# Values of heads 0 to 7 as products 512 columns wide, the second quarter of them kept on the chip

## The chip, the cores and the metric

The kernel runs on one core of a Trainium2 chip. A core has five engines, each with a queue of its own: TensorE (PE in the profile; its weight loads are listed apart as PEld), VectorE (DVE), ScalarE (ACT), GpSimd (POOL) and SyncE (SP, which here only starts transfers). Matrix products are accumulated in PSUM, eight banks of 512 float32 columns by 128 partitions; everything else lives in SBUF. The metric is the time of one execution on the device in microseconds (us); less is better. The profile is that of one execution, its times counted from the first instruction.

## The reference

One layer is applied to 128 prompt tokens and 512 latent tokens with the same weights, 1024 channels wide. Per token:

```
h = x * (1 + scale) + shift                       # modulation from the condition
z = h @ w_in                                      # 1024 -> 10240
v_h, x1, x0 : short convolution of z; y_h = (longconv(v_h * x1) + skip) * x0
q, k, v     : 16 heads of 64; prompt: full attention;
              latents: 2-D window plus the cached context keys, one softmax
p_h = (y_h * silu(g_h)) @ w_bh;  p_a = (y_a * silu(g_a)) @ w_ba
out = (sigmoid(m_h) * p_h + sigmoid(m_a) * p_a) @ w_out
x_new = layer_norm(alpha * x + gate * out)
```

Outputs are the new tokens of both groups and the prompt's keys and values (new_k, new_v). The change concerns `v = h @ w_v`, 640 tokens by 1024 columns, of which 64 columns are one head.

## The kernel before

**Precision.** Every float32 operand of a large product is split in a high part, rounded to the type that TensorE takes at full rate, and the low rest. A product is three products: high by high, low by high, high by low. The tokens are `hH` and `hL` (eight tiles of 128 channels by 640 tokens each), the weights `wh` and `wl`.

**Weight supply.** A weight tile is 128 partitions by 1024 columns (512 KB). `wtile` (L144) makes one ready: SyncE loads it into a ring `raw` of three; ScalarE writes its negative, rounded, into `wl` (L156, ring of three); GpSimd starts a second transfer of the same tile that adds to `wl` (L157), which leaves the rest with its sign; ScalarE writes `wh` (L158, ring of two). A ring's next tile is written only when the last reader of the old one is done.

**Stages.** Projections for the long convolution and the convolution itself (in four quarters) come first, then what the code calls the hand-over, then attention, whose query, key, gate and mixing weights go through `pair_tile` (a scheme with seven products of half size, L1167), then the output projections and the normalisation. The hand-over, `hand_over` (L943), makes the last gated convolution rows, then the values of all heads and the first query and key tile. Beside it runs the last quarter's long convolution (transforms `long_conv`, `long_conv_back`, and `gated_conv`, which ends with transposes `y`), then `attention_setup` (L956), which frees the convolution's memory and opens attention's, then `late_sums` (L793), sums of token tiles that `pair_tile` takes as operands. `weave` (L73) interleaves the two in the order in which they are written into the program: a piece of the side after so many pieces of the main, at 81 main pieces to 28 side pieces.

**Who orders what.** In the hand-over a planner orders every engine's instructions: it simulates the program with its own costs and sends ahead what is ready. From attention on (the block that opened with `values_back(1)` at L1335) TensorE's order is that of the program, and the planner orders the others. Each engine takes its queue in order.

**Values.** `values(m)` (L898) makes four heads, 256 columns, for m = 0 to 3. For each of eight channel tiles it multiplies the stationary token tile (128 channels by 128 tokens) with 256 weight columns, for five tiles of 128 tokens and three products: 120 products of 256 columns, at L917 (token tiles 0 to 3, two to a PSUM bank) and L929 (token tile 4). PSUM is used through two pools of four banks, `acc` (main, L104) and `aux` (L101), each handed out in turn. ScalarE copies the sums out (L924: two of 512 columns; L931: one of 256). For m = 0 they go to the place from which attention reads them, `slot(0, "v")`. The place of m = 1, in the pool `slots_r`, is only opened after the hand-over (L1280); those of 2 and 3 are still in use by others until far into attention. So m = 1, 2, 3 are copied into the room of the first keys (`k`, `kl` of `slots_l`), stored to DRAM (`v_d`, three transfers each), and read back by `values_back(m)` (L937): m = 1 at the start of attention, ahead of the first load of the output gate's weights (`gate_load`), the others later. The order of the hand-over is values 1, 2, 3, queries 0, keys 0, values 0.

The first use of a value in attention is well after its start: the first blocks compute scores (L979) and softmax first.

Of the kernel before, what the change touches and what calls it, by code (L numbers as in the profile page):

```python
# [11 lines left out]
AF = mybir.ActivationFunctionType  # L12
# [34 lines left out]
def tile_hyena_natten_step(ctx: ExitStack, tc: tile.TileContext, a, o):  # L47
# [751 lines left out]
    def alongside(main, side, every, first=0):  # L799
        for i, _ in enumerate(main):  # L800
            if i >= first and i % every == 0:
                next(side, None)
            yield
        for _ in side:
            pass

    at = sp = tp = None

    with tc.manual_schedule(engines={mybir.EngineType.PE, mybir.EngineType.DVE, mybir.EngineType.Activation}):
        prologue()  # L810
# [22 lines left out]
    def slot(j, tag, name, dt=F32):  # L833
        pool = out["slots_l" if j % 2 == 0 else "slots_q" if tag[0] == "q" else "slots_r"]
        return pool.tile([P, SLOT[tag]], dt, tag=tag, name=name)
# [62 lines left out]
    def values(m):  # L898
        w = [wtile(T_V + 2 * m + i, "dma", width=256) for i in range(2)]
        ps = [acc(f"v{m}_{i}") for i in range(2)]  # L900
        if m:
            v = [slot(0, t, f"v{m}{t}")[:, :n] for t, n in (("k", 512), ("kl", 768))]
            v = [v[0], v[1][:, :512], v[1][:, 512:]]
        else:
            out["v0"] = slot(0, "v", "v0")
            v = [out["v0"][:, 512 * i : min(512 * i + 512, 1280)] for i in range(3)]

        def passes(k):
            wh, wl = w[k // 4][0][k % 4], w[k // 4][1][k % 4]
            return ((hH, wh, k == 0, False), (hL, wh, False, False), (hH, wl, False, k == NK - 1))  # L910

        for half in range(2):
            ks = range(4 * half, 4 * half + 4)
            for k in ks:
                for x, wk, first, last in passes(k):
                    for t in range(4):
                        nc.tensor.matmul(  # L917
                            ps[t // 2][:, t % 2 * 256 : t % 2 * 256 + 256], x[:, k, P * t : P * t + P], wk,
                            start=first and t % 2 == 0, stop=last, skip_group_check=True,
                        )  # L920
                yield
            if half:
                for i in range(2):
                    nc.scalar.activation(v[i], ps[i][:], AF.Copy)  # L924
            else:
                pe = acc(f"ve{m}")
            for k in ks:
                for x, wk, first, last in passes(k):
                    nc.tensor.matmul(pe[:, :256], x[:, k, P * 4 :], wk, start=first, stop=last, skip_group_check=True)  # L929
            yield  # L930
        nc.scalar.activation(v[2], pe[:, :256], AF.Copy)  # L931
        nc.sync.dma_start(o["new_v"][:, m * 256 : m * 256 + 256], v[0][:, :256])
        for i in range(3 if m else 0):
            nc.sync.dma_start(v_d[m][:, 512 * i : min(512 * i + 512, 1280)], v[i])
        yield

    def values_back(m):  # L937
        out[f"v{m}"] = slot(m, "v", f"v{m}")
# [4 lines left out]
    def hand_over():  # L943
        nonlocal tp
        yield from quarter_tail(3)
        hwa_stack.close()
        out["slots_l"] = left.enter_context(tc.tile_pool(name="slots_l", bufs=1))
        out["slots_q"] = left.enter_context(tc.tile_pool(name="slots_q", bufs=1))
        tp = left.enter_context(tc.tile_pool(name="tp", bufs=1))
        yield from alongside(chain(values(1), values(2), values(3), queries(0), keys(0), values(0)), early_sums(), 1)  # L950

    tail = ctx.enter_context(ExitStack())
    ac = ctx.enter_context(ExitStack())
    edges, biases = {}, {}

    def attention_setup():  # L956
        nonlocal at, sp
        while "early_sums" not in out:
            yield
        hy.close()  # L960
        sp = ac.enter_context(tc.tile_pool(name="sp", bufs=1, side="right"))
        at = ac.enter_context(tc.tile_pool(name="at", bufs=1, side="right"))
        biases[0] = [bias_tile(h) for h in range(2)]
        for b, c in ((0, 0), (3, 320)):
            for h in range(2):
                edges[b, h] = at.tile([P, 384], F32, tag=f"edge{b}{h}", name=f"edge{b}{h}")
                nc.gpsimd.memset(edges[b, h][:, c : c + 64], 0.0)
        yield
# [273 lines left out]
    def mix_(m):  # L1242
# [10 lines left out]
    GATED_AT = [runs[0][i][0] for i in (0, 1, 2, 3, 5, 6, 7, 8, 10, 11, 12, 13, 15, 16, 17, 18)]  # L1253

    weave(hand_over(), chain(gated_conv(2), long_conv(3), long_conv_back(3), gated_conv(3), attention_setup(), late_sums()),
          4 * NK + 3 * N_VALUES + 16, 2 * N_GATED + N_CONV + N_BACK + 7)
    gp = left.enter_context(tc.tile_pool(name="gp", bufs=1))
    gbc = gp.tile([P, 2, D], F32, tag="gbc", name="gbc")

    gate_raw, gate_n = {}, [0]  # L1260
# [7 lines left out]
    def gate_row(after):  # L1268
# [6 lines left out]
        behind(ins, after)  # L1275
        tc.keep_in_program_order(ins)
        gate_n[0] += 1

    rs = left.enter_context(ExitStack())
    out["slots_r"] = rs.enter_context(tc.tile_pool(name="slots_r", bufs=1))  # L1280

    def yh_home(i):
        if i < 4:
# [48 lines left out]
        }[j]  # L1332

    with tc.manual_schedule(engines={mybir.EngineType.PE}):
        values_back(1)  # L1335
        before = last[0]
        gate_load()
        behind(last[0], before)
        for j in range(8):
            main, n_main = mains(j)  # L1340
            if j in (3, 5):
                values_back(j // 2 + 1)
            weave(chain(*main), attend(j), n_main, N_ATT if j < 7 else N_ATT + 3, 1 if j in (2, 4, 6) else 0)
# [284 lines left out]
def _layout(inp):  # L1628
    g = {n: np.asarray(v) for n, v in inp.items()}
    x = np.concatenate([g["x_prompt"][0], _to_blocks(g["x_sample"][0])], axis=0)  # L1630

    def ktiles(w):
        n = w.shape[1] // 128
        return w.reshape(8, 128, n, 128).transpose(2, 1, 0, 3).reshape(n, 128, 1024)

    w_in = g["w_in"][0]
    w_v = w_in[:, 48 * 128 : 56 * 128].reshape(2, 4, 128, 4, 256).transpose(3, 0, 2, 1, 4).reshape(8, 128, 1024)
    wall = np.concatenate(
        [ktiles(w_in[:, : 48 * 128]), w_v, ktiles(w_in[:, 56 * 128 :]), ktiles(g["w_bh"][0]), ktiles(g["w_ba"][0]), g["w_out"][0].reshape(8, 128, 1024)], axis=0)
    b_ada = g["b_ada"][0]  # L1640
    w3 = g["filt_w3"][0].reshape(64, 2, 4, 256).transpose(0, 2, 1, 3).reshape(64, 4, 512)
    b1, b2 = g["filt_b1"][0], g["filt_b2"][0]
    fr = g["filt_freq"][0]
    fs2 = np.stack([b2, fr[1]], axis=1)
    w2 = g["filt_w2"][0]
    convw = np.concatenate([g["conv_w"][0], g["conv_b"]], axis=0).reshape(4, 24, 128).transpose(2, 1, 0)
    p, n = np.arange(128)[:, None], np.arange(256)[None]
    ri = (n % 64) // 8 - (p % 64) // 8 + 7
    ci = np.clip((n // 64) * 8 + n % 8 - 8 - (p // 64) * 8 - p % 8 + 15, 0, 30)
    rpbT = g["rpb"][0][:, ri, ci]  # L1650
    half, qc8 = np.arange(128) // 64, np.arange(128) % 8
    qc = half * 8 + qc8
    bias = np.zeros((16, 128, 1024))
    for w, lo, r0, cols in (
        (24, np.maximum(qc - 8, 0), 64, (slice(0, 192),)), (32, qc, 0, (slice(320, 448), slice(576, 704))),
        (24, 8 + np.minimum(qc - 8, 0), 0, (slice(832, 1024),)),
    ):
        j = np.arange(8 * w)
        key = (j // 64) * 8 + j % 8
        ok = (key[None] >= lo[:, None]) & (key[None] < lo[:, None] + 16)  # L1660
        part = np.where(ok[None], rpbT[:, :, r0 : r0 + 8 * w], -BIG)
# [15 lines left out]
    return {n: np.ascontiguousarray(v) for n, v in out.items()}  # L1677
# [33 lines left out]
```

## Time and profile before

| | |
|---|---|
| median of three runs | 863.28 us (860.81 to 864.22) |
| the profiled execution | 860.83 us |
| its span (first to last instruction) | 859.1 us |
| granted clock of TensorE, mean | 0.998 of full |
| products of `values`, first and last start | 298.1 and 382.3 us (L917, L929) |
| values(0), the last part of the hand-over | 368.3 to 382.4 us |

In a list of groups or of instructions, `v<-wl,hH` is output and inputs; `128*128 128x256` is the shape of a product, here 128 channels by 128 tokens stationary and 256 columns moving; `x128` is the count. A product's duration is from its start to the modelled end of its results; products overlap, so the distance between starts tells what one costs in a row of them. A bracket at a line's end is the time for which the engine sat idle before it and what ended that. In the chain of work that ended last each piece carries only the time that it added. A queue's own row (SPq) is the issue of a transfer, not the transfer.

### The profile page before, as it was taken

Reading aid. Unit: us, or ns where it says so; the run is one execution under the profiler, and the core shown is the slowest. Engines: PE = TensorE matmul, PEld = TensorE weight load, DVE = VectorE, ACT = ScalarE, POOL = GpSimd, SP = SyncE. Lnnn points to the kernel's source line nnn. Section 1 sums busy time; section 2 is a strip of 40 time slices with the busy share of each in tenths; the row PEclk is TensorE's granted clock in tenths of the full one; section 3 lists DMA queues with packets and bytes.
Section 4 is the critical chain, followed back from the end, with each engine's and each line's share of the span. In section 5 each row is a group of like instructions: output and inputs, shape, how many; then the busy total and the mean of one; then the engine's idle time right before and its main releaser. Section 6 shows DMA issues by size and latency. Waiting matters only on the chain.

```text
span 859.1 us, 16817 instructions
## 1 busy us (share of the span) xinstructions
PE 849.4 (99%) x6387; PEld 822.7 (96%) x6387; DVE 678.7 (79%) x1408; ACT 464.7 (54%) x996; POOL 131.4 (15%) x140
## 2 busy tenths in 40 slices
PE   9999999999999999999999999999999999999996
PEld 7999999999999999999999999999999999999885
DVE  6777695697759559789988897889888778799776
ACT  4675656545554643646665676666655654345310
POOL 0010010101001010105232225124222200000000
PEclk9999999999999999999999999999999999999999
DMA  9986575656657558774263535354354386445621
GB/s 352 359 256 144 109 149 126 153 122 144 127 134 150 126 146 187 168 251 148 85 195 90 192 95 189 106 177 149 105 173 118 111 266 202 173 131 140 246 107 54
DMA packets 56868, 138.64 MB, mean 161 GB/s; under 512 B 8495, under 2 KB 23859, under 8 KB 56788
## 3 DMA queue, kind: packets, MB, share of 16 engines
q1 hardware_dynamic: 45412, 111.69, 39.7%
q0 software_dynamic: 5760, 20.19, 14.4%
q10 hardware_dynamic: 5616, 5.70, 1.9%
q8 instruction: 50, 0.82, 0.4%
q14 instruction: 30, 0.25, 0.1%
HBM read 121.43 MB, written 16.12 MB: 160 GB/s over the span
## 4 chain that ended last, share of the span: by engine, by line
PE 95%; DMA 3%; DVE 1%; SPq 0%; ACT 0%; issue 0%; DVEq 0%
PE sp L1182 33%; PE mm L177 30%; PE out L1534 6%; PE v L917 5%; PE pt L1019 3%; PE s L1026 3%; PE s L979 2%; PE mm L191 2%; PE ve L929 1%; DMA raw<-wall 1%; DMA wl<-wall 1%; DMA ada<-wada 1%; PE adaT L262 1%; PE yb L166 1%; PE yb L165 1%; PE yb L167 1%
## 5 line engine op out<-in xcount | busy, mean ns | idle before, releaser
L1182 PE MATMUL sp<-t,wb 128*128 128x320 f32 x912 | 141.7, 310 | 0.0
L1182 PEld LDWEIGHTS sp<-t,wb 128*128 128x128 f32 x912 | 134.9, 188 | 0.9 <-ACT pp L1047 0.5
L1182 PE MATMUL sp<-hH,wb 128*128 128x320 f32 x456 | 111.2, 314 | 0.0
L177 PE MATMUL mm<-hH,wl 128*128 128x320 f32 x448 | 105.5, 309 | 0.1
L177 PE MATMUL mm<-hH,wh 128*128 128x320 f32 x448 | 104.9, 309 | 0.0
L177 PE MATMUL mm<-hL,wh 128*128 128x320 f32 x448 | 104.2, 310 | 0.0
L157 POOL DMA_DIRECT2D wl<-wall x37 | 32.2, 870 | 329.5 <-ACT wl L156 263.3
L108 ACT ACTIVATE wb<-s 128x512 fp32r<-128x512 f32 x92 | 56.3, 627 | 45.6 <-DVE s L1142 26.6
L1182 PEld LDWEIGHTS sp<-hH,wb 128*128 128x128 f32 x456 | 78.4, 188 | 2.3 <-issue 2.1
L158 ACT ACTIVATE wh<-raw 128x1024 fp32r<-128x1024 f32 x37 | 39.2, 1059 | 70.8 <-PE mm L177 65.3
L177 PEld LDWEIGHTS mm<-hH,wl 128*128 128x128 f32 x448 | 75.5, 188 | 0.9 <-DMA wl<-wall 0.4
L177 PEld LDWEIGHTS mm<-hH,wh 128*128 128x128 f32 x448 | 75.2, 188 | 0.5
L177 PEld LDWEIGHTS mm<-hL,wh 128*128 128x128 f32 x448 | 75.1, 188 | 0.3
L109 DVE TENSOR_TENSOR wb<-s,wb 128x512 fp32r<-128x512 f32 x92 | 62.5, 692 | 10.3 <-ACT wb L108 10.3
L1182 PE MATMUL sp<-hL,wb 128*128 128x320 f32 x228 | 70.4, 309 | 0.0
L108 ACT ACTIVATE wb<-raw 128x512 fp32r<-128x512 f32 x66 | 41.4, 628 | 44.4 <-PE sp L1182 23.5
L1001 POOL TENSOR_SCALAR p<-p,sm 128x384 f32<-128x384 f32 x32 | 44.5, 1399 | 102.7 <-DVE sm L1000 102.7
L109 DVE TENSOR_TENSOR wb<-raw,wb 128x512 fp32r<-128x512 f32 x66 | 46.6, 705 | 5.5 <-ACT wb L108 5.4
L177 PE MATMUL mm<-yhs,wh 128*128 128x320 f32 x256 | 47.9, 309 | 0.0
L1197 DVE TENSOR_TENSOR c<-sp,u 128x320 f32<-128x320 f32 x69 | 33.5, 486 | 12.0 <-PE sp L1182 12.0
L1182 PEld LDWEIGHTS sp<-hL,wb 128*128 128x128 f32 x228 | 42.8, 188 | 0.0
L1001 POOL TENSOR_SCALAR edge<-edge,sm 128x320 f32<-128x320 f32 x32 | 41.9, 1318 | 0.5 <-DVE sm L1000 0.5
(385 smaller groups left out, 2078.3 us busy)
## 6 DMA issues: line engine op xcount, KB each, us to landing
raw<-wall SPq DMA_DIRECT2D x93, 512.0 KB, 3.6
wl<-wall POOLq DMA_DIRECT2D x37, 512.0 KB, 5.8
ada<-wada SPq DMA_DIRECT2D x16, 512.0 KB, 9.2
tm<-bias SPq DMA_DIRECT2D x16, 512.0 KB, 4.5
xw<-xw SPq DMA_DIRECT2D x8, 512.0 KB, 9.4
gate<-wgate SPq DMA_DIRECT2D x8, 512.0 KB, 4.1
wo<-wall SPq DMA_DIRECT2D x8, 512.0 KB, 5.3
dec<-decay SPq DMA_DIRECT2D x20, 128.0 KB, 3.0
```

Of the source, the lines that this page charges most:

```text
L108: hi = nc.scalar.activation(dst_h, src, AF.Copy)
L109: return hi, (eng or nc.vector).tensor_tensor(dst_l, src, f(dst_h), op=ALU.subtract)
L157: nc.gpsimd.dma_start(wl, a["wall"][i], accum_op=ALU.add)
L158: nc.scalar.activation(wh, raw[:], AF.Copy)
L177: nc.tensor.matmul(ps[hf][:, :HALF], wt[k], x[:, hf * HALF : (hf + 1) * HALF], start=(i == 0 and k == 0), stop=(i == lead[2] and k == NK - ...
L917: nc.tensor.matmul(ps[t // 2][:, t % 2 * 256 : t % 2 * 256 + 256], x[:, k, P * t : P * t + P], wk, start=first and t % 2 == 0, stop=last, ...
L1001: nc.gpsimd.tensor_scalar_mul(pv, pv, sm[:, 2:3])
L1019: nc.tensor.transpose(pt[:, i * P : i * P + P], x, ident)
L1026: nc.tensor.matmul(dst, lhs, rhs, start=start, stop=stop, skip_group_check=True)
L1182: nc.tensor.matmul(dst, wk, x(xi, k), start=j < 4 and k == 0 and i == 0, stop=k == 3 and i == 2, skip_group_check=True,)
L1197: after = nc.vector.tensor_tensor(c, dst, c if j == 3 else u, op=ALU.add)
L1534: ins = nc.tensor.matmul(dst, m[k][:, c0 : c0 + P], w[:, c : c + n], start=(first and k == 0), stop=(last and k == 5), skip_group_check=True,)
```

## The change

`values` stays for m = 2 and 3 only. A new part, `first_values`, at the end of the hand-over, makes heads 0 to 7 (512 columns) at once: four weight tiles hold two channel tiles by 512 columns each (the host lays out the weights so), and for each weight tile and each of five token tiles there are six products of 512 columns: two channel tiles by three. The five sums stay open in PSUM through all four weight tiles, four in the main pool's banks and one in an `aux` bank; after the last weight tile's products for a token tile, ScalarE copies its two halves to the places of m = 0 and m = 1. For this, `slots_r`, and `gp` (the output gate's rows) which lies before it in memory, are opened in `attention_setup`, within the hand-over. The stores of m = 1 to DRAM and its load go. The weave's ratio is again 81 to 28 (written as a number), but the main part now has its last 20 pieces in `first_values`, of which 9 lie past the 81, where before the 11 pieces of values(0) did.

```diff
     def values(m):
         w = [wtile(T_V + 2 * m + i, "dma", width=256) for i in range(2)]
         ps = [acc(f"v{m}_{i}") for i in range(2)]
-        if m:
-            v = [slot(0, t, f"v{m}{t}")[:, :n] for t, n in (("k", 512), ("kl", 768))]
-            v = [v[0], v[1][:, :512], v[1][:, 512:]]
-        else:
-            out["v0"] = slot(0, "v", "v0")
-            v = [out["v0"][:, 512 * i : min(512 * i + 512, 1280)] for i in range(3)]
+        v = [slot(0, t, f"v{m}{t}")[:, :n] for t, n in (("k", 512), ("kl", 768))]
+        v = [v[0], v[1][:, :512], v[1][:, 512:]]
...
-        for i in range(3 if m else 0):
+        for i in range(3):
             nc.sync.dma_start(v_d[m][:, 512 * i : min(512 * i + 512, 1280)], v[i])
         yield
+
+    def first_values():
+        ps = {}
+        for kt in range(4):
+            w = wtile(T_V + kt, "dma", width=512)
+            for t in range(5):
+                if kt == 0:
+                    ps[t] = acc(f"v_{t}") if t < 4 else aux("ve")
+                for n, (x, i, kk) in enumerate(((hH, 0, 0), (hL, 0, 0), (hH, 0, 1), (hL, 0, 1), (hH, 1, 0), (hH, 1, 1))):
+                    nc.tensor.matmul(
+                        ps[t][:], x[:, 2 * kt + kk, P * t : P * t + P], w[i][kk],
+                        start=kt == n == 0, stop=kt == 3 and n == 5, skip_group_check=True,
+                    )
+                if kt == 3:
+                    while "slots_r" not in out:
+                        yield
+                    for m in range(2):
+                        if t == 0:
+                            out[f"v{m}"] = slot(m, "v", f"v{m}")
+                        v = out[f"v{m}"][:, 256 * t : 256 * t + 256]
+                        nc.scalar.activation(v, ps[t][:, 256 * m : 256 * m + 256], AF.Copy)
+                        if t == 0:
+                            nc.sync.dma_start(o["new_v"][:, m * 256 : m * 256 + 256], v)
+                yield
...
-        yield from alongside(chain(values(1), values(2), values(3), queries(0), keys(0), values(0)), early_sums(), 1)
+        yield from alongside(chain(values(2), values(3), queries(0), keys(0), first_values()), early_sums(), 1)
...
     def attention_setup():
...
         at = ac.enter_context(tc.tile_pool(name="at", bufs=1, side="right"))
+        gp = left.enter_context(tc.tile_pool(name="gp", bufs=1))
+        rs = left.enter_context(ExitStack())
+        out["slots_r"] = rs.enter_context(tc.tile_pool(name="slots_r", bufs=1))
...
-          4 * NK + 3 * N_VALUES + 16, 2 * N_GATED + N_CONV + N_BACK + 7)
-    gp = left.enter_context(tc.tile_pool(name="gp", bufs=1))
+          81, 2 * N_GATED + N_CONV + N_BACK + 7)
...
-        values_back(1)
-        before = last[0]
         gate_load()
-        behind(last[0], before)
```

More of the change, by code (lines that the diff above doesn't have):

```diff
@@ L805, in alongside @@
             pass
-    at = sp = tp = None
+    at = sp = tp = gp = rs = None
     with tc.manual_schedule(engines={mybir.EngineType.PE, mybir.EngineType.DVE, mybir.EngineType.Activation}):
@@ L956, in attention_setup @@
     def attention_setup():
-        nonlocal at, sp
+        nonlocal at, sp, gp, rs
         while "early_sums" not in out:
@@ L1277, in gate_row @@
         gate_n[0] += 1
-    rs = left.enter_context(ExitStack())
-    out["slots_r"] = rs.enter_context(tc.tile_pool(name="slots_r", bufs=1))
     def yh_home(i):
@@ L1636, in _layout @@
     w_in = g["w_in"][0]
-    w_v = w_in[:, 48 * 128 : 56 * 128].reshape(2, 4, 128, 4, 256).transpose(3, 0, 2, 1, 4).reshape(8, 128, 1024)
+    w_v = w_in[:, 48 * 128 : 56 * 128]
+    w_v = np.concatenate(
+        [w_v[:, :512].reshape(4, 2, 128, 512).transpose(0, 2, 1, 3).reshape(4, 128, 1024),
+         w_v[:, 512:].reshape(2, 4, 128, 2, 256).transpose(3, 0, 2, 1, 4).reshape(4, 128, 1024)], axis=0)
     wall = np.concatenate(
```

## The prediction

> **What bounds the kernel now.** I read the page first (engine totals, then the chain that ended last), then the waits of the matmul engine, then the chain and the stretches around the edit, and last the instructions of each engine there in order of time.
>
> The page's first lines and the engines' shares of the chain:
>
> ```profile
> span 859.1 us, 16817 instructions
> PE 849.4 (99%) x6387; PEld 822.7 (96%) x6387; DVE 678.7 (79%) x1408; ACT 464.7 (54%) x996; POOL 131.4 (15%) x140
> ...
> PE 95%; DMA 3%; DVE 1%; SPq 0%; ACT 0%; issue 0%; DVEq 0%
> ```
>
> All the waits of the matmul engine in the whole span (engine, line, waited for: us, times, longest):
>
> ```profile
> PE mm L281 <- DVE hid L273: 1.2, 1, 1.2
> PE adaT L262 <- DMA ada<-wada: 0.6, 2, 0.3
> ```
>
> TensorE is the bound: 99% busy, 95% of the chain. Its two waits lie in the opening at L262 and L281; in the hand-over there is none. So the edit can gain only what it takes out of TensorE's own work, and any wait it creates goes into the total one for one. The stretches from the first value product to some way into attention (length, busy time and count by engine, granted clock, DMA share, GB/s):
>
> ```profile
> 298.00:351.00 53.00, 53.00 (x450) 52.91 (x449) 39.50 (x66) 25.77 (x43) 5.20 (x6) 1.00 0.71 166
> 351.00:368.20 17.20, 17.20 (x126) 17.19 (x125) 13.12 (x29) 10.52 (x19) 2.12 (x6) 1.00 0.79 164
> 368.20:382.40 14.20, 14.20 (x122) 14.20 (x121) 11.62 (x21) 6.09 (x14) 0.00 (x0) 1.00 0.85 313
> 382.40:420.00 37.60, 37.60 (x292) 36.15 (x291) 34.02 (x97) 24.90 (x71) 13.67 (x13) 1.00 0.41 129
> ```
>
> TensorE has no gap in any of them and runs at the full granted clock; VectorE and ScalarE have 2.6 and 8.1 us to spare in the 14.2 us before attention.
>
> **The change, part by part.** *1. Product width.* 240 products 256 columns wide become 120 products 512 wide: same columns, half the instructions. The chain shows values(0) as four pieces (start, us), and the output stage at the end has 512-wide products back to back (start of 24, start of the next):
>
> ```profile
> 368.43 5.66 PE v L917 x48
> 374.09 1.41 PE ve L929 x12
> 375.50 5.65 PE v L917 x48
> 381.15 1.42 PE ve L929 x12
> ```
>
> ```profile
> 830.47 5.60 PE L1534 MATMUL out<-wo,yhs 128*128 128x512 f32 x24
> 835.91 0.39 PE L1534 MATMUL out<-woh,yhs 128*128 128x512 f32 x1
> ```
>
> A 256-wide product takes (381.15 + 1.42 - 368.43) / 120 = 117.8 ns, a 512-wide one (835.91 - 830.47) / 24 = 226.7 ns. 240 x 117.8 = 28.27 us become 120 x 226.7 = 27.20 us: **-1.1 us**. A pair of narrow products costs 235.6 ns, so nearly 9 ns for each instruction fewer is all that the halved count saves. The Trainium skill ("TensorE: Matmul & The Clock Gate", Back-to-back issue gap) puts a warm product at N / 2.4 + 2.5 ns, which gives as an estimate 109.2 and 215.8 ns and a saving of 120 x 2.5 = 0.3 us. The fixed part in this trace is more than three times that; by that rule the saving here is 0.3 us and the time 863.3.
>
> *2. Weight loads.* 120 loads fewer. One lasts 188 ns:
>
> ```profile
> L917 PEld LDWEIGHTS v<-wh,hH x128: 187/188/202, 297.9 to 379.8; 128*128 128x128 f32 x128
> ```
>
> Products start every 117.8 ns, less than one load lasts, so loads already run beside products and beside each other. I cost their removal at nothing beyond part 1; at 512 columns 226.7 ns of product cover 188 ns of load, so the cover stays.
>
> *3. The trip through DRAM for heads 4 to 7.* Three stores (640 KB) and one load (640 KB) go, with four issues of SyncE. The load, its size, and what stands behind it in that queue:
>
> ```profile
> 368.25 0.55 SPq L64 DMA_DIRECT2D v<-v_d  x1
> ...
> 370.47 0.58 SPq L64 DMA_DIRECT2D raw<-wall  x1
> ```
>
> ```profile
> v<-v_d SPq DMA_DIRECT2D x1, 640.0 KB
> ```
>
> ```profile
> 356.64 0.49 DVE L890 TENSOR_TENSOR kl<-ck,k 128x128 fp32r<-128x128 f32 x2 [0.92 <-DMA v_d<-v3kl]
> ```
>
> Between these two stand the first load of the output gate, the store of the new keys and the cached values; all of them can go out some 0.55 us sooner, and the weight load behind the stores likewise. Since TensorE waits for none of them, I take 0. The one wait on a store in this stage is VectorE's 0.92 us in the last row, on the values of heads 12 to 15, whose trip stays.
>
> *4. Evictions on ScalarE.* Before, a group of four heads takes two of 128x512 and one of 128x256:
>
> ```profile
> 380.95 1.09 ACT L924 ACTIVATE v<-v 128x512 f32<-128x512 f32 x2 [1.80 <-PE v L917]
> 382.54 0.63 ACT L108 ACTIVATE wb<-s 128x512 fp32r<-128x512 f32 x1 [0.50 <-ACT v L924]
> 383.07 0.36 ACT L931 ACTIVATE v<-ve 128x256 f32<-128x256 f32 x1
> 383.34 0.62 ACT L108 ACTIVATE wb<-raw 128x512 fp32r<-128x512 f32 x1
> ```
>
> That is 1.45 us a group, 2.9 us for two; after, ten of 0.36 us, 3.6 us, of which eight lie beside the last quarter's products and two behind the last one. ScalarE's 8.1 us of slack hide the 0.7 us more. Queued behind the last two are the splits of the next weights: the last ends 0.36 us later, at about 384.3, and its low half on VectorE at about 385:
>
> ```profile
> 383.20 0.69 DVE L109 TENSOR_TENSOR wb<-s,wb 128x512 fp32r<-128x512 f32 x1 [3.18 <-ACT wb L108]
> ```
>
> The first pair tile needs those weights only past its third of seven sums, the end of the 36 products that start at 385.86 (row in part 6), at 391. Cost 0; with that cover gone 0.4 us.
>
> *5. A fifth bank, out of the other pool.* Sums 0 to 3 take all four banks of the main pool, the fifth takes one of the four auxiliary banks, and all stay open through four weight tiles. Two things come late next. Sums 2 and 3 need keys(0)'s banks, whose last readers follow the end of keys(0) at 368.43 by 2.0 and 3.1 us:
>
> ```profile
> 369.75 0.62 DVE L885 TENSOR_TENSOR kl<-mm,k 128x64 fp32r<-128x64 f32 x3
> ...
> 371.01 0.56 DVE L885 TENSOR_TENSOR kl<-mm,k 128x64 fp32r<-128x64 f32 x2
> ```
>
> Sum 2 is reached after 12 products, 2.7 us, sum 3 after 4.1 us: 0.7 and 1.0 us of slack, so 0 if VectorE keeps this order, and 1 us if two token sums of 0.8 us (part 6) get ahead. The fifth sum's bank, counted round in the order of requests, is that of the last piece of the inverse transform, released by the first row here; the second row is the last transposes, and the third (a stretch, busy time and count of that transform's products alone) what of it is left after 351:
>
> ```profile
> 361.69 0.40 ACT L686 ACTIVATE E<-yb 128x256 f32<-128x256 f32 x1
> ...
> 365.05 1.03 PE L704 MATMUL y<-pack,E 128*128 128x128 f32 x8
> ```
>
> ```profile
> 351.00:366.00 15.00, 2.80 (x18) 1.00 0.77 167
> ```
>
> The new products end near 381.5 and so begin near 350.5 (less 27.2, less 2.8 and 1.0 us of transforms and transposes among them); the fifth sum comes after 24 x 0.227 = 5.4 us and some 1.5 us of transforms, near 357.4, and its bank at 361.69 + 0.40 = 362.1: 4.7 us too late, if the transforms keep their time. The order of TensorE here is the planner's; if it sends the next tile's four sums (5.4 us) ahead, this costs 0; if it keeps the order written, 4.7 us. Between these ends I take **+0.3 us**, near the lower one, since the stretches above show the planner filling such gaps with other products throughout.
>
> *6. Order.* Heads 8 to 15, queries and keys move some 14 us forward, the values of heads 0 to 7 become the only cover for the end of the side work (token sums on VectorE). Those are last written and first read here:
>
> ```profile
> 374.14 1.57 DVE L109 TENSOR_TENSOR t<-again_t,t 128x640 fp32r<-128x640 f32 x2
> ...
> 379.19 0.83 DVE L109 TENSOR_TENSOR t<-again_t,t 128x640 fp32r<-128x640 f32 x1 [0.20 <-ACT t L108]
> ```
>
> ```profile
> 384.27 0.33 PE L979 MATMUL s<-k,q 64*128 64x384 f32 x2
> ...
> 385.86 5.43 PE L1182 MATMUL sp<-t,wb 128*128 128x320 f32 x36
> ```
>
> From 375.71 to 385.86 the sum needed first has 10 us in hand; 1.1 us less changes nothing. Query and key evictions may now come ahead of the transforms on VectorE and delay them by 2 to 3 us, inside that slack. The second block of scores (384.27) takes the fifth sum's bank, free 2 x 0.36 us after the last product against 1.9 us: 0; with two 0.63 us splits in between, 0.1 us.
>
> **Sum.** -1.1 + 0.3 = -0.8 us. The profiled execution took 860.83 us, 1.7 beside its span and 2.45 below the median of 863.28; the same saving from the median gives **862.5 us**. The three runs spread over 3.4 us (0.4%), so 0.5%, 4.3 us, is about what a measurement tells from no change.
>
> **The rivals.**
> *A. The fifth bank stops TensorE* (slower than before). Against it: the planner had ready products at every moment of this stage; for it: the inverse transform's last eviction is only at 361.69, and until the fifth sum is through, the first tile's high weights stay held too. Price 4.7 us less the 1.1: 863.28 + 3.6 = 866.9. It decides as soon as a wait over 1.1 us stands before the fifth sum. Chance 0.2.
> *B. A new order for VectorE and ScalarE makes attention late*: splits or loads that met their moment miss it, in a stage where 34.0 of 37.6 us of VectorE are taken. Six waits of one 128x512 split (0.63 + 0.69 us) are 7.9 us, less the 1.1: 870. Chance 0.1.
> *C. The edit does not do what it says*: products of 512 with hH as weights go no faster per column: 863.3 to 863.6. The 512-wide rows of the output stage speak against it. Chance 0.06.
> *D. Weight loads do hold up products.* If each load were on the path, 120 x 0.188 = 22.6 us go: 840.7. The starts every 117.8 ns speak against it. Chance 0.01. The Trainium skill ("TensorE: Matmul & The Clock Gate", "What overlaps and what doesn't" under Part 3) states that a load overlaps running products only where the row group differs; here all loads take all 128 rows, and the trace does not agree.
> *E. Traffic was a hidden cost*: with 1.3 MB less, at the 313 GB/s of the stretch before attention 4.2 us, weights come sooner. No wait shows it. At most 863.28 - 1.1 - 4.2 = 858.0. Chance 0.03.
>
> **How the numbers follow.** The forecast (a saving up to 1.1 us, a wait under 1.1 us) has 0.6; its own range is 860.5 to 864.5, with the spread of the median. A reaches to 867, B beyond, E below. From 859.8 to 867.0 leaves out most of B, D, half of E and a tail of A, about 0.17. Slower by over 0.5% (above 867.6): nearly all of B and a quarter of A, 0.15. Faster by over 0.5% (below 859.0): D, most of E, 0.04. The rest, 0.81, is within.
>
> **What would show it.** Right: the new products start every 226 to 230 ns at full clock, no TensorE wait between 298 and 400, attention's first scores near 382.6, the load of v gone. Wrong: a gap before the fifth sum with a ScalarE releaser at the inverse transform's eviction (A); starts later than 230 ns apart (C); waits for splits or weight loads after 385 (B); a shift larger than 1.1 us at the hand-over's end (D, E).

## The result, and the profile after

| | before | after |
|---|---|---|
| median | 863.25 us (860.45 to 864.88) | 866.08 us (863.98 to 867.28) |
| ratio to before | | 1.0038, 95% interval 1.0025 to 1.0051 |
| profiled execution; its span | 860.83; 859.1 us | 867.28; 865.5 us |
| first product of the hand-over's values | 298.06 us | 301.19 us |
| from there to attention's first pair product (`sp`) | 84.34 us | 86.74 us |
| from there to attention's first transposes (`pt`) | 100.58 us | 103.41 us |
| from there to the end of the span | 561.04 us | 564.31 us |

The change made the kernel slower by 0.38%, 2.8 us, where 0.8 us less was forecast. The 13 executions spread over 4.4 us before and 3.3 after, and the two profiled ones differ by 3.13 us ahead of the first value product, where the order of the instructions is the same; so profiles are compared from that product on, in the last three rows. There the changed kernel loses 3.27 us: 2.40 before attention's first product, 0.43 in the next 17 us, 0.44 in the rest.

The page's first lines and the engines' shares of the chain, after:

```profile
span 865.5 us, 16574 instructions
PE 853.5 (99%) x6267; PEld 820.1 (95%) x6267; DVE 678.7 (78%) x1408; ACT 464.1 (54%) x1000; POOL 131.5 (15%) x140
...
PE 96%; DMA 2%; DVE 1%; ACT 0%; issue 0%; SPq 0%; DVEq 0%
```

TensorE is still the bound, busy for 99% of the span and 96% of the chain, so the loss must show as waits or as dearer products. All its waits:

```profile
PE sp L1205 <- ACT v L952: 2.1, 1, 2.1
PE mm L281 <- DVE hid L273: 1.2, 1, 1.2
PE yp L696 <- ACT E L686: 0.5, 1, 0.5
PE ps_f L228 <- DMA pack<-pack: 0.2, 1, 0.2
```

Two are new and lie in the changed stage (L281 and L228 belong to the opening): 0.5 us before the transposes `yp`, 2.1 us before attention's first pair product, for an eviction of the new sums. The stretches of that stage (length, busy time and count by engine, granted clock, DMA share, GB/s):

```profile
301.10:354.00 52.90, 52.90 (x420) 52.59 (x419) 38.87 (x70) 26.70 (x51) 5.21 (x6) 1.00 0.72 169
354.00:371.30 17.30, 16.83 (x93) 14.36 (x92) 13.21 (x29) 7.71 (x13) 1.26 (x5) 1.00 0.27 51
371.30:385.60 14.30, 14.30 (x64) 11.56 (x62) 8.67 (x13) 4.08 (x7) 0.86 (x1) 1.00 0.91 312
385.60:423.00 37.40, 35.27 (x269) 33.25 (x269) 34.73 (x89) 25.82 (x74) 12.09 (x10) 1.00 0.43 132
```

The second row is the surprise. Before, transfers took 0.79 of the 17 us ahead of the last stretch; now 0.27, and then all comes at once, at 0.91. Something held the transfers back. TensorE's instructions in order of time:

```profile
367.99 0.44 PE L696 MATMUL yp<-pack,E 128*128 128x128 f32 x2 [0.47 <-ACT E L686]
368.26 1.04 PE L704 MATMUL y<-pack,E 128*128 128x128 f32 x8
369.06 0.48 PE L941 MATMUL ve<-wh,hH 128*128 128x512 f32 x1
...
387.93 0.41 PE L1205 MATMUL sp<-hH,wb 128*128 128x320 f32 x1 [2.13 <-ACT v L952]
...
389.89 0.67 PE L1002 MATMUL s<-k,q 64*128 64x384 f32 x2
```

The fifth sum (`ve`) starts at 369.06, with the first weight tile's products, where sums 0 to 3 had theirs from 352.71 on. Until then the first two weight tiles can't be given back. ScalarE, which writes the next ones:

```profile
367.55 0.38 ACT L686 ACTIVATE E<-yb 128x256 f32<-128x256 f32 x1 [2.99 <-PE yb L167]
...
370.27 1.06 ACT L158 ACTIVATE wh<-raw 128x1024 fp32r<-128x1024 f32 x1 [0.47 <-PE ve L941]
371.24 1.04 ACT L156 ACTIVATE wl<-raw 128x1024 fp32r<-128x1024 f32 x1
...
385.56 1.15 ACT L108 ACTIVATE wb<-s 128x512 fp32r<-128x512 f32 x2 [6.37 <-DVE s L1165]
386.62 0.72 ACT L108 ACTIVATE t<-again_t 128x640 fp32r<-128x640 f32 x1
387.24 2.28 ACT L952 ACTIVATE v<-v 128x256 f32<-128x256 f32 x8
```

The third tile's `wh` is written when `ve` releases the ring, and only that frees a slot of `raw` for the weights of attention's first pair tile. SyncE's issues:

```profile
369.38 0.33 SPq L64 DMA_DIRECT2D tm<-bias  x1
...
371.24 0.94 SPq L64 DMA_DIRECT2D gate<-wgate  x1
372.29 0.40 SPq L64 DMA_DIRECT2D raw<-wall  x1
```

By then attention's own first loads, two of `tm` and one of `gate` (512 KB each), and two stores of the convolution's rows (`yh_d`, 320 KB each) stand ahead, and VectorE gets the weights late:

```profile
382.89 0.69 DVE L1165 TENSOR_TENSOR s<-raw,raw 128x512 f32<-128x512 f32 x1 [3.88 <-DMA raw<-wall]
```

VectorE stood still for 3.88 us, ScalarE for 6.37 us behind it, and the ten evictions of the values (two a sum, 2.28 us for the first eight) stood in ScalarE's queue behind the two splits and the split of a token sum. TensorE waited for the first of them. The chain of work that ended last goes the same way:

```profile
372.29 10.58 DMA raw<-wall
...
382.89 0.69 DVE s L1165
...
386.71 0.63 ACT t L108
387.34 0.55 ACT v L952 x2
...
387.93 1.15 PE sp L1205 x6
```

This is a reading of one trace; the experiments test its links.

### The profile page after: what moved, and what is told of

It is laid out like the page before. It is cut to its first block, busy times and chain, and to the rows that moved or that the text cites. A ratio compares the mean times of both kernels' runs of the same rounds, so it can differ in the third digit from the quotient of the medians.

```text
span 865.5 us, 16574 instructions
## 1 busy us (share of the span) xinstructions
PE 853.5 (99%) x6267; PEld 820.1 (95%) x6267; DVE 678.7 (78%) x1408; ACT 464.1 (54%) x1000; POOL 131.5 (15%) x140
## 4 chain that ended last, share of the span: by engine, by line
PE 96%; DMA 2%; DVE 1%; ACT 0%; issue 0%; SPq 0%; DVEq 0%
PE sp L1205 33%; PE mm L177 32%; PE out L1550 6%; PE pt L1042 3%; PE v L913 3%; PE s L1049 3%; PE s L1002 2%; PE mm L191 2%; PE v L941 1%; DMA raw<-wall 1%; PE adaT L262 1%; PE ve L925 1%; PE yb L165 1%; PE yb L166 1%; PE yb L167 1%; PE ut L611 1%
```

## The experiments

For comparison, from the first value product of each profiled execution on (us). The medians were taken at different times, with the kernel before beside them at 861.6 to 863.3 us; the ratios, each to the kernel before of the same time, are what can be compared.

| kernel | to `sp` | to `pt` | to the end | median | ratio to before (95%) |
|---|---|---|---|---|---|
| before | 84.34 | 100.58 | 561.04 | | |
| after | 86.74 | 103.41 | 564.31 | 866.08 | 1.0038 (1.0025 to 1.0051) |
| narrow, both straight | 84.35 | 100.57 | 561.69 | 862.36 | 1.0003 (0.9986 to 1.0020) |
| bank one piece earlier | 83.77 | 100.36 | 561.02 | 861.56 | 0.9989 (0.9975 to 1.0004) |
| the same, fifth sum first | 84.31 | 100.64 | 561.42 | 862.36 | 1.0000 (0.9984 to 1.0016) |
| the same, fifth sum second | 83.77 | 100.08 | 561.04 | 861.97 | 1.0001 (0.9989 to 1.0012) |
| after, fifth sum first | 86.94 | 103.27 | 564.04 | 865.85 | 1.0040 (1.0023 to 1.0057) |
| control: bank late again | 86.91 | 103.58 | 564.45 | 866.58 | 1.0040 (1.0023 to 1.0056) |
| first piece's bank | 83.87 | 100.11 | 562.34 | 864.14 | 1.0018 (1.0003 to 1.0032) |
| the same, fifth sum second | 83.87 | 100.11 | 562.36 | 863.18 | 1.0012 (0.9997 to 1.0027) |
| after, gate load later | 84.45 | 105.77 | 566.78 | 867.93 | 1.0072 (1.0050 to 1.0094) |
| after, evictions first | 86.41 | 104.63 | 565.61 | 867.83 | 1.0057 (1.0035 to 1.0079) |
| both of these | 86.13 | 104.30 | 565.23 | 867.37 | 1.0052 (1.0035 to 1.0069) |
| after, raw weights first | 84.46 | 102.01 | 562.71 | 863.21 | 1.0019 (1.0000 to 1.0038) |

**Narrow products, both quarters straight to their places.** All of the change but the width: 256 columns, `values(1)` and `values(0)` last, no fifth sum across weight tiles.

```diff
-        yield from alongside(chain(values(2), values(3), queries(0), keys(0), first_values()), early_sums(), 1)
+        yield from alongside(chain(values(2), values(3), queries(0), keys(0), values(1), values(0)), early_sums(), 1)
```

> The products of heads 0 to 7 are 256 columns wide again, as values(1) and values(0) at the end of the hand-over; both go straight to their places, without the trip through DRAM, and no fifth sum stays open through four weight tiles: all else of the change stays (order, memory opened early). Theory H (the fifth sum of the wide products gets its bank late, holds the weight tiles of the first two quarters, and all that follows is late): 863.2 us (862.5 to 864.0), no wait of TensorE for an eviction at the hand-over's end. Rival O (the cost lies in the order: heads 0 to 7 are the only work left beside the end of the long convolution, whatever their width): 866, with TensorE waits of 2 us or more between 350 and 395.

Measured: 862.36 us, just under the expected range, the same as before, and no wait for an eviction. So the new order, the memory opened early and the trip through DRAM that went together cost and bring nothing that can be measured (the interval reaches 0.2% to either side); the loss sits in the wide products and their sums. The chain shows the narrow products at an unchanged price, 5.65 / 48 = 117.7 ns in the same stage:

```profile
355.44 3.18 PE v L914 x27
...
371.89 5.65 PE v L914 x48
```

**The fifth sum's bank one piece earlier.** Which auxiliary bank a sum gets is settled when the program is built. In the changed kernel's trace the fifth sum starts only behind the eviction of the inverse transform's last piece (367.55), which fits that piece's bank, as the prediction had counted. When `yp` writes into the free half of that piece's bank, the fifth sum should get the second piece's; in this kernel's trace it starts at 364.1, ahead of the last piece's eviction (365.72).

```diff
             pb = aux(f"yb{q}_{g}")
+            if q == 3 and g == 2:
+                out["yp3"] = pb[:, 256:]
...
-        outp = aux(f"yp{q}")
+        outp = out["yp3"] if q == 3 else aux(f"yp{q}")
```

> As the changed kernel, but the transposes yp write into the unused half of the last inverse-transform bank. The auxiliary banks are handed out in turn, so the fifth sum moves one bank on, from that of the inverse transform's last piece to that of its second piece, which is evicted 4.2 us earlier (363.3 against 367.6 in the changed kernel's profile). Nothing else changes. Theory H: the fifth sum starts near 366.5 instead of 369.1, fills the 0.6 us wait before yp, and frees the two weight tiles some 2.5 us sooner: 0.6 us and about half of the 2.1 us wait at the end go, 864.4 us (863.5 to 865.3). Rivals W (width itself, or the ten evictions on ScalarE) and O (order): 866.0, within 0.5, with the wait at the end as long as before.

Measured: 861.56 us, lower than expected; both waits are gone, and the whole loss with them. SyncE's issues in this kernel:

```profile
367.08 0.33 SPq L64 DMA_DIRECT2D raw<-wall  x1
368.00 0.33 SPq L64 DMA_DIRECT2D tm<-bias  x1
...
370.87 1.37 SPq L64 DMA_DIRECT2D gate<-wgate  x1
```

Now the weights go out first, 69.30 us after the first value product against 71.10, ahead of `tm`. VectorE has them at 371.91, 74.1 us after that product against 81.7:

```profile
371.91 0.69 DVE L1167 TENSOR_TENSOR s<-raw,raw 128x512 f32<-128x512 f32 x1 [1.40 <-DMA raw<-wall]
```

So 1.8 us at the issue became 7.6 us at the use, most of it on the way: 10.6 us from issue to use against 4.8. (The low weights of the fourth tile are used last of all in both kernels, in eight products from 383.34 and from 379.25, so the five sums end together in both; that alone makes no wait.) With no wait left, this kernel also shows the price of the wide products (start, us, count, from the chain):

```profile
352.64 4.44 PE v L943 x19
...
359.89 3.50 PE v L943 x15
...
367.97 5.49 PE v L943 x24
...
374.84 3.66 PE v L943 x16
```

That is 233.7, 233.3, 228.8 and 228.8 ns. All twelve pieces of these products, the fifth sum's included, add up to 27.66 us for 120 products, 230.5 ns each.

**The order of the token tiles.** In the last weight tile 4, 0, 1, 2, 3 in place of 0 to 4, with the bank earlier, and alone:

```diff
-            for t in range(5):
+            for t in range(5) if kt < 3 else (4, 0, 1, 2, 3):
```

> As the kernel with the fifth sum's bank one piece earlier, and in the last weight tile the token tiles in the order 4, 0, 1, 2, 3 instead of 0 to 4. Theory H: as without the new order or up to 0.5 us less, 864.1 us (863.3 to 865.2), since the sums still all wait for the same last low weights. A rival by which the order of the evictions makes the wait at the end: 863.5 or less, with the 2.1 us wait for v gone.

> The changed kernel with one edit: in the last weight tile the token tiles come in the order 4, 0, 1, 2, 3. Theory H: 866.0 us, within 0.5 of the changed kernel, since the low weights of that tile still come last for all five sums. The rival by which the order of the evictions makes the wait: 864.0 to 865.0, with the 2.1 us wait shortened by 1 us or more.

Measured: 862.36 us, lower than expected, and 865.85 us, as expected. With the late bank the wait for `v` stays, at 2.3 us; with the early one a wait of 0.4 us comes up, since the sum whose bank the pair tile takes is finished second. The order is not the cause. But from the first pair product to the first pair tile's next products it is 2.57 and 2.56 us here, against 2.90 in the changed kernel, 2.81 with the bank alone and 2.48 before: the second block of scores takes the fifth sum's bank, and its eviction comes last. So the best of both should be the order 0, 4, 1, 2, 3:

> The kernel with the fifth sum's bank one piece earlier, and in the last weight tile the token tiles in the order 0, 4, 1, 2, 3, so that the sum whose bank the first pair tile takes is still finished first, and the one whose bank the second block of scores takes is finished second. Its profile with the order 0 to 4 shows the first pair tile with no wait, but 2.81 us from there to its second block (2.48 in the kernel before); with the order 4, 0, 1, 2, 3 it was 2.57 us after a wait of 0.38. Theory: no wait for v, and some 0.25 us less than with the order 0 to 4, 0.8 us below the kernel before from the hand-over's first product to the end (560.2 to 560.8 us of 561.0): faster than both kernels, by 0.1% of the kernel before. Rival (the rest of attention takes back what the hand-over saves): 561.0 or more, no difference to the kernel before.

Measured: the wait is gone, the stretch is 2.54 us, and 0.5 us is won up to the first transposes (100.08). At the end nothing of it is left (561.04), and the time, 861.97 us, can't be told from the kernel before. The expectation of 560.2 to 560.8 was missed.

**A control.** The kernel with the bank one piece earlier also sends the transposes `y` ahead. So the same with the fifth sum in the bank that the last piece and `yp` share (`out["ve"]`), which is free late:

```diff
-                    ps[t] = acc(f"v_{t}") if t < 4 else aux("ve")
+                    ps[t] = acc(f"v_{t}") if t < 4 else out["ve"]
```

> The control to the kernel with the fifth sum's bank one piece earlier: again the transposes yp write into the unused half of the last inverse-transform bank, and the large transposes y go ahead of that piece as there, but the fifth sum is put in that same bank, so that it has to wait for the last piece's eviction, the transposes yp and VectorE's reading of them, as late as in the changed kernel or later. Theory H (the late bank is the cause): slow again, 865.5 to 867.0 us against some 861.6 to 862.4, with TensorE waits of 2 us or more between 360 and 395. Rival (moving the transposes was what helped): within 0.5 us of the kernel with the earlier bank, about 862.

```profile
PE sp L1207 <- ACT v L954: 1.4, 1, 1.4
PE mm L281 <- DVE hid L273: 1.2, 1, 1.2
PE yb L943 <- DVE yh L708: 0.6, 1, 0.6
PE yb L698 <- ACT E L688: 0.5, 1, 0.5
```

Measured: 866.58 us. (`yb L943` is the fifth sum here.) Two kernels whose programs differ only in the fifth sum's bank stand at 1.0040 and 0.9989 of the kernel before, and 3.4 us apart from the first value product on: the late bank is the cause. (Here the fifth sum also has to wait until VectorE has read `yp`.)

**The first piece's bank.** As `out["ve"] = pb` at the inverse transform's first piece, `yp` in a bank of its own; and the same with the order 0, 4, 1, 2, 3:

> The changed kernel with the fifth sum put in the bank of the inverse transform's first piece (evicted at 356.5 us in the changed kernel's profile, 11 us before the last piece's); the transposes yp keep a bank of their own. Theory H: no wait of TensorE from the hand-over's first product on, 561.0 us from there to the end as with the second piece's bank, median 861.5 to 862.5. That the bank comes 7 us earlier still should bring nothing more, since no wait was left. Rival (the gain came with the shared bank and its order, not with the time of the bank): 865 to 866.

> The same with the token tiles of the last weight tile in the order 0, 4, 1, 2, 3, so that the bank that the scores take is given back sooner. Theory: 0.2 to 0.4 us less from the hand-over's first product to the first transposes of attention (100.0 to 100.2 us, against 100.58 in the kernel before); median 861.2 to 862.2, not told apart from the kernel before by the times. Rival: a wait for an eviction returns in another place, 862.5 or more.

Measured: 864.14 and 863.18 us. Both are above what was expected. Up to `pt` the gain is there (100.11), but 1.8 us are lost behind it, and the expectation of no wait fell:

```profile
372.50 0.38 PE L698 MATMUL yp<-pack,E 128*128 128x128 f32 x2
...
406.19 1.73 PE L1207 MATMUL sp<-t,wb 128*128 128x320 f32 x10 [1.03 <-DVE wb L109]
```

With the bank so early the planner sends the fifth sum and the third weight tile ahead of the side work: `yp` comes 73.8 us after the first value product, against 66.8 before. VectorE's work on the side's end starts that much later, and at 406 TensorE waits 1.0 us for a weight split of VectorE's. That the one makes the other was not tried apart. By this reading the bank must be free in time, but products sent ahead of `y` take the cover from the side work. Of the three banks the one in between came out best here.

**Which link makes the 2.1 us?** Four kernels keep the late bank and change only orders. The gate's first load behind the raw weights (called six pieces into attention's first pair tiles):

> The changed kernel, but the first load of the output gate's weights (512 KB, first used some 10 us into attention) is called six pieces into attention's first pair tiles, so that in SyncE's queue it stands behind the load of the pair tile's second raw weights and not ahead of it. Nothing else moves; TensorE's order is the same, and the fifth sum's bank is as late as in the changed kernel. Theory T (the late bank costs its 2.1 us at the end because the raw weights freed late stand behind attention's loads, land late, and the splits that wait for them stand ahead of the evictions on ScalarE): the raw weights land 1 to 1.7 us sooner (512 KB at 312 GB/s), the wait of 2.1 us for v falls to 1.1 or less, and the median to 864.3 to 865.2 us, by 0.9 to 1.8 under the changed kernel's 866.1; the wait before yp (0.5) stays. Rival U (the five sums end late because the fourth tile's low weights land late, or the ten evictions themselves make the wait): 866.0 within 0.5, the wait as long as before.

Measured: VectorE has the weights 79.6 us after the first value product, 2.1 us sooner, though they were issued at the same moment (71.1), and the first pair product waits for nothing (84.45). But one late split now stood between the evictions, and the second block of scores waited 3.1 us for the fifth sum's bank: 867.93 us. The expected time was missed by 3 us, the link from the transfers to the first wait held, and the rival, by which the sums or their ten evictions make that wait whatever the transfers do, did not. Behind that wait the clock fell (see the last section).

The first two splits of the late weights behind the evictions on ScalarE, alone and with the gate's load later:

```diff
+                if "evicted" in out and j in (1, 2):
+                    behind(high[i0, j], out["evicted"])
```

> The changed kernel with one order fixed on ScalarE: the first two splits of the pair tile's late weight sums (which waited until 385.56 us in the changed kernel's profile) come behind the ten evictions of the values, not ahead of them. The fifth sum's bank and the raw weights stay late. Theory S (the 2.1 us wait for v is made by splits that wait for late raw weights, ahead of the evictions in one queue): the wait for v before the first pair tile goes, the granted clock does not drop behind it in any execution; part comes back as a wait for the second weight sum, some 0.5 to 1 us, since that is split later; 864.0 to 865.3 us against 866.1. Rival (the sums themselves end too late for the evictions): the wait for v stays at 1.5 us or more, 866.

> Both edits: the evictions ahead of those splits on ScalarE, and the output gate's first load behind the pair tile's raw weights in SyncE's queue. Alone, the later gate brought the raw weights 2.1 us sooner and took away the first wait, but the evictions then stood apart, with a split that waited between them, and the scores waited 3.1 us. Theory S: no wait for v and none over 0.5 us for a split; the wait before yp (0.5) is what is left: 863.0 to 864.2 us, within 0.2% of the kernel before, the mean clock at 0.997 or more in all executions. Rival (the wait before yp or the late weights cost by themselves): 865 or more.

Measured: 867.83 and 867.37 us. Both are above what was expected, and theory S fell: the wait for `v` stays at 1.8 and 1.5 us, and 1.2 us for a split come on top. ScalarE's instructions in the second kernel say why:

```profile
383.06 0.74 ACT L108 ACTIVATE t<-again_t 128x640 fp32r<-128x640 f32 x1 [6.79 <-DVE again_t L739]
383.71 2.29 ACT L952 ACTIVATE v<-v 128x256 f32<-128x256 f32 x8
```

With the two splits out of the way the evictions stand behind the split of a token sum, which waits for VectorE, and VectorE had stood still for the raw weights (4.21 us until 377.94). It is not one instruction of ScalarE that is late but VectorE's whole queue, with which ScalarE takes turns.

So the last one: the two loads of `tm` called behind the first piece of attention's pair tiles, and so behind the raw weights; the gate's load still goes out ahead of those, and bank and kernel are else as changed.

```diff
-        biases[0] = [bias_tile(h) for h in range(2)]
...
+                if i == 0:
+                    biases[0] = [bias_tile(h) for h in range(2)]
+                    gate_load()
```

> The changed kernel with one order changed among transfers: attention's first two bias loads (tm, 1 MB) are called behind the pair tile's raw weights and not ahead of them; the gate's load still stands ahead. The fifth sum's bank and ScalarE's program are as in the changed kernel, though the planner may order ScalarE and VectorE anew with the weights expected sooner. Theory T (the late bank costs most of its time because the raw weights, freed late, share the queues and the bandwidth with attention's first loads, and VectorE, which takes its queue in order, stands still until they land): they land 2 to 3.4 us sooner (up to 1 MB at 312 GB/s), VectorE's wait of 3.9 us for them falls under 1.5, TensorE's wait for v of 2.1 us under 0.5; 863.5 to 864.8 us against 866.1, the wait before yp (0.5) stays. Rival (with the bank that late, the time is lost whatever the transfers do): a wait of 1.5 us or more stands before 400 us again, 866 or more.

```profile
PE mm L281 <- DVE hid L273: 1.2, 1, 1.2
PE s L1001 <- ACT v L952: 0.9, 1, 0.9
PE yp L696 <- ACT E L686: 0.5, 1, 0.5
```

Measured: 863.21 us, below what was expected, but with the kernel before at 862.49 beside it: the ratio is 1.0019 against the changed kernel's 1.0038. VectorE has the weights 77.4 us after the first value product, 4.4 us sooner; its wait for them is still 2.86 us, not under 1.5, but ends that much sooner. The 2.1 us are gone; 0.5 us for `yp` and 0.9 us for the fifth sum's bank are left, and the first transposes come 1.4 us later than before, against 2.8 in the changed kernel. So with the bank as late as in the changed kernel, another order of the transfers takes about half of the loss away: 1.60 of the 3.27 us from the first value product on, and half by the ratios, whose intervals overlap. That half the late bank cost by way of the weight rings and SyncE's queue, not by the products that waited for it; the other half is still there. The planner set ScalarE and VectorE anew in this kernel, so the shares of transfer and order are not measured apart.

No version here measurably beats the kernel before. A third buffer for `wh`, which might have let the rings run on, wasn't tried.

## Why the prediction was wrong

*1. Product width: mis-sized.* -1.1 us was the term; the wide products took 230.5 ns and not 226.7 (kernel with the bank one piece earlier), 27.66 us and not 27.20, so the saving is 0.6 us. That kernel, which has no wait, has its first pair product 0.57 us earlier than the kernel before, which agrees. The Trainium skill ("TensorE: Matmul & The Clock Gate", Back-to-back issue gap), by whose rule, stated there for the isolated gap of one product, 0.3 us were to be had, is off to the other side. The output stage was the wrong row to take a price from for another stage.

*2, 3. Weight loads, the DRAM trip: right as far as shown.* Nothing beyond the 0.6 us came with 120 loads fewer, and the narrow kernel has the new places without the trip and takes the time of before.

*4. Evictions: wrong.* "Cost 0" looked only at splits queued behind the evictions. In the trace the evictions stood behind splits, and those behind VectorE. The 0.7 us more of eviction did not matter (the kernel with the bank one piece earlier has the same ten and no wait); their place in the queue did.

*5. The fifth bank: this is the step that failed.* Its bank was named rightly, and the direct wait came out near what was taken: 0.5 us against +0.3, because the planner did send the next tile's four sums ahead. But the term priced only TensorE's own wait. That the first weight tiles stay held until the fifth sum is through was written down under rival A and given no price: `wh` of the third tile 370.27, a raw slot free after it, the load behind `tm` and `gate`, VectorE 3.88 us idle, and 2.13 us of TensorE at the end. That the bank's time is the cause, the control shows; that about half of the loss goes by the order of the transfers, the kernel with raw weights first; the path on ScalarE and VectorE is read from the trace and was not settled apart. One more link was mis-sized: the last piece's eviction came 66.4 us after the first value product against 63.6 before. That is the delay of 2 to 3 us which part 6 allowed for the transforms; part 5 counted with the bank as if they kept their time. How much of the loss that makes was not tried.

*6. Order: right that no pair product waits for a token sum, mis-sized behind.* The second block of scores lost 0.42 us (2.90 against 2.48) where 0 to 0.1 was given.

The account from the first value product: width -0.6; before `yp` 0.6 (0.47 of it for the releaser); before the first pair product 2.3 (2.13); that makes 2.3 of the 2.40. The scores take 0.4. The last 0.44 us, behind the first transposes, have no pattern: that stretch takes 460.5 us before, 460.9 after, 460.7 with the bank one piece earlier and 461.1 in the narrow kernel.

*Rivals.* A named the mechanism, and its time (866.9) is near the measured one by luck: its condition, a wait over 1.1 us before the fifth sum, never held, and the price was paid 18 us later, by another route. B's form (splits and loads that miss their moment) is how it was paid. C is half true: 230.5 ns for 512 columns against 235.4 for twice 256. D and E are out: no weight loads held up products, and the narrow kernel, which has less traffic too, gained nothing (1.0003).

## What to carry to other kernels

A sum that stays open across weight tiles holds those tiles until its own bank is free; price that by following the ring to the next load, and the load to its place in the queue, and not by the wait of the sum itself. A free moment for a transfer is worth more than its length: 1.8 us later at the issue was 7.6 us later at the use, because it fell behind three loads of 512 KB and two stores of 320 KB. When an edit takes away slack on a busy core, look for the two in-order queues that take turns (here VectorE and ScalarE): moving one instruction out of the way only shows the next one.

## What the runs showed of the hardware

One wait of TensorE cost more than its length. Behind the wait of 3.15 us in the kernel with the gate's load later, the granted clock fell to half for 3.4 us (stretch, then busy times, clock, DMA share, GB/s):

```profile
384.90:388.00 3.10, 0.06 (x1) 0.00 (x0) 2.05 (x5) 3.10 (x11) 0.00 (x0) 1.00 0.00 0
388.00:389.00 1.00, 0.90 (x5) 0.72 (x5) 0.61 (x3) 1.00 (x6) 0.00 (x0) 0.61 0.28 33
389.00:390.00 1.00, 1.00 (x6) 0.74 (x4) 1.00 (x4) 0.53 (x3) 0.00 (x0) 0.50 0.79 229
390.00:391.00 1.00, 1.00 (x5) 1.00 (x5) 1.00 (x6) 0.39 (x2) 0.62 (x2) 0.50 0.88 307
391.00:392.00 1.00, 1.00 (x6) 1.00 (x6) 0.20 (x3) 0.73 (x2) 1.00 (x2) 0.68 0.81 205
392.00:393.00 1.00, 1.00 (x9) 1.00 (x8) 0.69 (x1) 1.00 (x4) 0.64 (x1) 1.00 0.54 217
```

0.39 + 0.50 + 0.50 + 0.32 = 1.7 us of full speed, 3.4 us at half, were lost after 3.15 us of waiting. The Trainium skill ("TensorE: Matmul & The Clock Gate", What's actually happening) puts the clock at half after an idle window of some 3.4 us, and back to full after as long a busy one; the half and the 3.4 us agree, and here 3.15 us of idle time were enough. Behind the 2.13 us of the changed kernel's profiled execution the clock stayed at 1.00, but the mean clock of five of its 13 executions was 0.995 or less, where the profiled one had 0.998. Part of its median may be this, but not the main part: its eight executions at 0.997 or 0.998 have a median of 865.4 us, still 2.1 above the kernel before. In the changed kernel with the fifth sum first, which waited 2.33 us, the five executions at 0.998 took 864.1 to 864.5 us and the seven at 0.993 to 0.996 865.6 to 869.0. But a low clock in the opening lowers that mean too (0.61 from 8 to 16 us, mean 0.994, in the profile of the kernel with the bank earlier and the fifth sum second), and none of the slow-clocked executions of these two kernels was profiled, so where they lost their clock stays open.

A 512-column product cost 233.3 to 233.7 ns in most of the stage with the inverse transform and 228.8 behind it (kernel with the bank one piece earlier), at a granted clock of 1.00 in both, while the 256-column ones of the narrow kernel stayed at 117.7. No run shows why.
